# Keys in one tile, score products of up to 512 columns and another order of the head pairs in a streaming-encoder step

## The chip, the cores and the metric

The kernel runs on one core of one Trainium2 chip. The metric is device time in microseconds (us) of one execution; each kernel is run several times and the median is compared.

## What is computed

One layer of a streaming encoder, for a prompt of 1024 frames and a sample group of 64 frames, with 1024 model dimensions. The parts that the change touches are the two attentions behind the first projection:

```python
h = rms_norm(xp, g_norm1[l])
qa, ka, va, qb, kb, vb, logf = in_proj(h, w_in[l], b_f[l], g_qa[l], g_ka[l], g_qb[l], g_kb[l])
oa = chunk_band_attn_prompt(qa, ka, va, rel_bias[l])   # 8 heads: own 64-frame chunk + 8 before it, relative bias
ob = forget_attn_prompt(qb, kb, vb, logf)              # 8 heads: causal, bias = cum[t] - cum[s], cum = cumsum(logf)
xp = xp + jnp.concatenate([oa, ob], axis=-1) @ w_o[l]
```

Both are softmax(q k / 8 + bias) v with heads of 64 dimensions. After them come a cross attention into 256 memory tokens, whose keys and values are projected in this kernel, and a feed-forward block with a short convolution. The sample group goes through the same layer with cached keys and values. The normalised keys, the values, the gates' logarithms and the memory's keys and values are outputs too.

## The kernel before, in words

**Precision.** TensorE works on a rounded 32-bit type (F32R). To keep precision, each operand is split into a high part (rounded) and a low part (the rest). A projection is three products: high x high, low x high, high x low (`SPLIT`, or `TERMS` at the start). In the attention, head dimension 64 leaves half of the 128 rows of the array free. So a query tile holds the high part of the query in one half of the partitions and its low part in the other. The key tile has two planes (`z` or `m` = 0 and 1, high and low), each with the same keys in both halves. The second half is filled by a DMA from the first (line 485, `k<-k`). A score is then two products, one per plane. For the values, high and low stand side by side as 128 weight columns (`v[:, j, h]` is 2 x 64), and the result has 128 rows, whose two halves are added at the end (lines 743 and 744).

**Stages.** The 16 heads go in 8 pairs, in the order `PAIRS` (line 24): pairs 0 to 3 are band attention ("local"), 4 to 7 forgetting attention. For each pair, the projection runs over eight blocks of 128 frames (line 407, 24 products of 384 columns each), then once over the sample group (line 529). Between these products the attention of earlier blocks is woven in, up to one pair late: `substeps` hands out the scores of one unit, the values of the unit before and the turning of new queries and keys. A unit (`Attn`) is one head and 256 queries (two blocks `j`) of one group of keys `g`. When the last pair's projection has ended, its last units run beside the projection of the memory (line 802); then follow the samples' attention (class `Sample`, in the order `SAMPLES`, line 25), the output projection and the rest of the layer (lines 1156, 1445, 1481, 1703, 2027).

**Keys and values.** Two blocks make a `Group` (lines 330 to 334), whose key tile has 256 columns per plane and head. The pool holds five such tiles. `group_turn` (line 473) transposes queries and keys and writes the key planes (ScalarE line 482, VectorE line 484, DMA line 485).

**Scores** (`score`, line 659). For query block t the window of key blocks is the five newest for a local pair and all t + 1 for a forgetting pair, that is up to 640 or 1024 columns of the PSUM tile `S` of two banks. The products (line 682) go group by group with 256 columns, or 128 where the window begins or ends in the middle of a group. Then come: add the bias and find the row's extreme (VectorE line 685), the exponential with its sum (ScalarE line 687), division by the sum (GpSimd line 689). In forgetting pairs GpSimd prepares the bias first (lines 667, 668).

**Values** (`turn`, `sum`, lines 705 and 723). The probabilities are transposed (line 719) and split (lines 720, 721). A block in the window of both query blocks is multiplied with 256 columns, a block in only one of the windows with 128; `self.full` lists the former. Line 734 does high and low probabilities with all 128 value columns.

**Gates' sum** (`forget`, line 558). The running sum of the logarithms of the gates is a scan over the frames, with eight heads on eight partitions (line 602), for the prompt and for the sample with its cache. Its pieces are handed out from block 1 of pair 1 on (line 867). Pairs 4 to 7 need its result as bias (line 639) and per query (line 612).

**The order of instructions.** Everything up to the first product of the feed-forward part (`arranged`, line 1591) is put in order by a planner, `arrange` (line 2050). It goes through the instructions as the program lists them, gives each a price (`cost`, line 2077) and plans every engine and SyncE's queue of DMAs. An instruction can be planned when what it needs is done; of those that are ready, the one earliest in the program goes first. `before` holds what has to be done, `starts` what has to have begun. The result is only an order on each engine. What an instruction waits for on the chip is set by the data alone. All DMAs are issued by SyncE.

Of the kernel before, what the change touches and what calls it, by code (L numbers as in the profile page):

```python
# [15 lines left out]
P = 128  # L16
# [6 lines left out]
NF = 22  # L23
PAIRS = (0, 1, 2, 3, 4, 5, 6, 7)
SAMPLES = (4, 7, 5, 6, 0, 1, 3, 2)
# [16 lines left out]
def hybrid_step(ctx: ExitStack, tc: tile.TileContext, i: dict, o: dict):  # L42
# [285 lines left out]


    class Group:  # L330
        def __init__(self):
            self.k = wa.tile([P, 2, 2, 256], F32R, name="k", bufs=5)
            self.v = wa.tile([P, 2, 2, 2, 64], F32R, name="v", bufs=5)
            self.q = self.qk = None
# [223 lines left out]
    def forget():  # L558
# [36 lines left out]
        def scan(n):  # L595
            nonlocal lt, cs
            cs = wk.tile([P, N], F32, name="s", bufs=4)
            if n == N:
                lt = wk.tile([P, N], F32, name="s", bufs=4)
                nc.sync.dma_start(lt[:8, 0:T], i["clogf"])  # L600
                dve.tensor_copy(lt[:8, T:N], ls)
            dve.tensor_tensor_scan(cs[:8, :n], lt[:8, :n], lt[:8, :n], 0.0, op0=ALU.add, op1=ALU.bypass)
            dve.tensor_scalar(lt[:8, :n], cs[:8, :n], -1.0, None, op0=ALU.mult)
            nc.sync.dma_start(negc if n == T else negs, lt[:8, :n])
# [37 lines left out]
    mixes = {}  # L642

    class Attn:

# [13 lines left out]
        def score(self, j, sp=None):  # L659
# [11 lines left out]
            else:  # L671
                b = bias[p, h][:, 640 - n:640]
            if sp is None:
                sp = ps.tile([P, 2, 512], F32, name="S", bufs=1).rearrange("p a b -> p (a b)")
            off = (w0 % 2) * P
            q = groups[p, g].q[:, h, j * P:(j + 1) * P]
            for kg in range(w0 // 2, t // 2 + 1):
                k0, k1 = max(w0, 2 * kg), min(t, 2 * kg + 1) + 1
                a = off + (k0 - w0) * P
                src = slice((k0 - 2 * kg) * P, (k1 - 2 * kg) * P)  # L680
                for m in range(2):
                    pe.matmul(sp[:, a:a + (k1 - k0) * P], q, groups[p, kg].k[:, h, m, src], start=m == 0, stop=m == 1)  # L682
            mx = wk.tile([P, 1], F32, name="mx", bufs=4)
# [39 lines left out]
        def sum(self, ch):  # L723
# [5 lines left out]
            op = self.op  # L729
            for b in sorted(ch, key=lambda b: (b != self.full[0], b)):  # L730
                cols = slice(0 if b <= a1 else 1, 2 if b >= b0 else 1)
                hi, lo, x = self.pts[b]
                for m, pt in enumerate((hi, lo)):
                    pe.matmul(op[:, cols], groups[p, b // 2].v[:, b % 2, h].rearrange("p a d -> p (a d)"),  # L734
                              pt[:, x, cols], start=b == self.full[0] and m == 0, stop=b == self.last and m == 1)
            if ch[-1] != self.last:
# [107 lines left out]
    for p, np_ in zip(PAIRS, PAIRS[1:] + (None,)):  # L844
# [5 lines left out]
        for t in range(NT):  # L850
# [13 lines left out]
            if t == 0:  # L864
                subs = extra[:1] + subs[:2] + extra[1:] + subs[2:]
                extra = []
            elif forgetting:
                subs += forgetting.pop(0)
# [1177 lines left out]

ENGINES = ("PE", "DVE", "Activation", "Pool", "SP")


def arrange(tc, end):  # L2050
# [6 lines left out]
    setter = select = None  # L2057
    held, slots = [], {}

# [17 lines left out]
    def cost(ins, engine, kind, cols, rows, psum):  # L2077

        op = str(getattr(ins, "op", ""))
        if engine == "PE":  # L2080
            if getattr(ins, "is_transpose", False):
                return 0.109, 0.35, False
            if ins.ins[0].bass_ap.dtype == F32:
                o = max(0.214, cols * 0.00178)
            else:
                o = max(0.087, 0.003 + cols * 0.000456)
            return o, o + 0.16, False
# [19 lines left out]
    for ins in traced[:end]:  # L2107
# [57 lines left out]
        if engine == "Pool":  # L2165
# [6 lines left out]
            elif kind == "InstTensorScalarAffineSelect":  # L2172
                select = n
        before.discard(n)
        nodes.append((ins, engine, before, starts, *cost(ins, engine, kind, cols, rows, psum)))
        held.append((olds, mine))

# [164 lines left out]
```

## Time and profile before

| | |
|---|---|
| median of the runs | 1707.46 us (3 runs, 1704.11 to 1709.73) |
| the profiled execution | 1703.21 us |
| its span, first to last instruction | 1701.4 us |
| mean clock granted to TensorE | 0.998 of full |

PE is TensorE, PEld its weight loads, DVE VectorE, ACT ScalarE, POOL GpSimd, SP SyncE; SPq and the like are an engine's sequencer, which waits or issues DMAs. L407 is line 407. A group of instructions is written as line, engine, operation, output<-inputs by the program's names, shape and count; for a product, 128*128 is the weights' rows and columns and 128x384 the moving operand. Behind the bar stand the busy time in us, the mean duration of one in ns, and the engine's idle time just before them with what ended it. Products overlap, so their durations say less than the distance between their starts. The chain of work that ended last follows the run back from its end, at each step to what released it; its pieces are given as start, length and what it is.

### The profile page before, as it was taken

To read this page: it belongs to the slowest core of one execution; us is meant where nothing else is said; L and a number is where in the kernel's file an instruction comes from. 1 tells how busy PE (TensorE), PEld (TensorE's weight loads), DVE (VectorE), ACT (ScalarE), POOL (GpSimd) and SP (SyncE) were. 2 spreads that over 40 slices of the span, in tenths; PEclk is the share of its full clock that TensorE was granted. 3 is DMA by queue.
4 is the path that set the end of the run, shared out by engine and by line. 5 is a ranking of instruction groups with operands and counts; after the bars stand their busy time and mean duration, and the time that the engine had idled before them with its cause. 6 is when DMAs were issued, how large, how long until landed. Compare 5 with 4: busy or idle time off the path is not lost.

```text
span 1701.4 us, 33544 instructions
## 1 busy us (share of the span) xinstructions
PE 1676.9 (99%) x12264; PEld 1636.4 (96%) x12264; DVE 1158.1 (68%) x2552; ACT 906.8 (53%) x1995; POOL 583.3 (34%) x846
## 2 busy tenths in 40 slices
PE   8999999999999999999999999999999999999999
PEld 8899999999998889999999999999999999999998
DVE  7877766767777645334444697777777777659986
ACT  8757766767777565335555554333333333434442
POOL 1746647888877104434445211000000000000000
PEclk9999999999999999999999999999999999999999
DMA  8322223223146955411114642222222222983332
GB/s 258 101 57 81 75 81 103 76 77 99 48 147 189 267 186 185 139 57 51 55 58 141 211 134 83 80 78 79 77 77 77 77 79 82 306 305 122 104 108 88
DMA packets 138422, 199.84 MB, mean 117 GB/s; under 512 B 22200, under 2 KB 77624, under 8 KB 138256
## 3 DMA queue, kind: packets, MB, share of 16 engines
q1 hardware_dynamic: 138256, 197.70, 37.8%
q8 instruction: 96, 1.57, 0.4%
q14 instruction: 70, 0.57, 0.1%
HBM read 148.01 MB, written 43.34 MB: 112 GB/s over the span
## 4 chain that ended last, share of the span: by engine, by line
PE 83%; DVE 6%; ACT 5%; DMA 2%; issue 2%; POOL 1%; SPq 0%; DVEq 0%; ACTq 0%; POOLq 0%
PE W L1703 26%; PE pj L1156 14%; PE W L2027 11%; PE pj L407 11%; PE S L682 4%; PE O L734 3%; PE PT L719 3%; PE pj L802 2%; PE W L1156 2%; PE pj L529 1%; PE S L1445 1%; PE tq L1481 1%; PE O L1481 1%; PE O L1056 1%; ACT q L487 1%
## 5 line engine op out<-in xcount | busy, mean ns | idle before, releaser
L407 PE MATMUL pj<-whi,xhi 128*128 128x384 f32 (+1 forms) x480 | 175.4, 365 | 0.0
L407 PE MATMUL pj<-wlo,xhi 128*128 128x384 f32 (+1 forms) x480 | 164.7, 343 | 0.0
L407 PE MATMUL pj<-whi,xlo 128*128 128x384 f32 (+1 forms) x480 | 164.1, 342 | 0.0
L1703 PE MATMUL W<-h,hi 128*128 128x272 f32 x704 | 134.3, 288 | 1.4 <-ACT qlo L1839 1.4
L1809 POOL COPY s<-gp 128x2 f32<-128x2 f32 x22 | 15.8, 719 | 336.1 <-DVE gp L1808 336.1
L2027 PE MATMUL W<-f,hi 128*128 128x272 f32 x672 | 127.2, 287 | 0.1
L721 DVE TENSOR_TENSOR ptl<-PT,pth 128x512 fp32r<-128x512 f32 (+2 forms) x192 | 98.5, 521 | 37.1 <-ACT pth L720 34.4
L720 ACT CAST pth<-PT 128x512 fp32r<-128x512 f32 (+2 forms) x192 | 85.2, 450 | 57.9 <-PE PT L719 55.8
L689 POOL TENSOR_SCALAR s<-s,ssum 128x640 f32<-128x640 f32 (+7 forms) x128 | 92.0, 720 | 69.5 <-DVE ssum L688 59.2
L687 ACT ACTIVATE s<-s,mx 128x640 f32<-128x640 f32 (+7 forms) x128 | 94.4, 737 | 37.6 <-DVE mx L685 36.9
L1703 PEld LDWEIGHTS W<-h,hi 128*128 128x128 f32 x704 | 110.4, 188 | 1.7 <-ACT qlo L1839 1.6
L2027 PEld LDWEIGHTS W<-f,hi 128*128 128x128 f32 x672 | 105.3, 188 | 0.3 <-DVE f L1774 0.3
L1703 PE MATMUL W<-h,lo 128*128 128x272 f32 x352 | 101.4, 288 | 0.0
L682 PE MATMUL S<-k,q 128*128 128x256 f32 (+1 forms) x608 | 94.3, 283 | 6.9 <-DVE mx L685 4.5
L682 PEld LDWEIGHTS S<-k,q 128*128 128x128 f32 x608 | 83.9, 190 | 17.2 <-DVE mx L685 5.6
L2027 PE MATMUL W<-f,lo 128*128 128x272 f32 x336 | 96.7, 288 | 0.0
L1566 ACT CAST hi<-raw 128x512 fp32r<-128x512 f32 x68 | 42.3, 621 | 98.8 <-PE W L1703 59.2
L719 PE MATMUL PT<-ident,s 128*128 128x128 f32 x528 | 89.8, 275 | 3.2 <-DVE ptl L721 1.5
L407 PEld LDWEIGHTS pj<-whi,xhi 128*128 128x128 f32 x480 | 90.9, 189 | 1.2
L407 PEld LDWEIGHTS pj<-wlo,xhi 128*128 128x128 f32 x480 | 91.2, 190 | 0.1
L407 PEld LDWEIGHTS pj<-whi,xlo 128*128 128x128 f32 x480 | 90.4, 188 | 0.0
L1156 PE MATMUL pj<-a,hi 128*128 128x384 f32 (+1 forms) x352 | 87.3, 332 | 1.0 <-DVE a L1209 0.9
(608 smaller groups left out, 5716.1 us busy)
## 6 DMA issues: line engine op xcount, KB each, us to landing
raw<-in_w_down_dram SPq DMA_DIRECT2D x45, 256.0 KB, 2.8
wraw<-in_w_dram SPq DMA_DIRECT2D x56, 192.0 KB, 2.7
raw<-in_w_up_dram SPq DMA_DIRECT2D x41, 256.0 KB, 2.7
h<-ad SPq DMA_DIRECT2D x32, 272.0 KB, 5.2
mwraw<-in_w_mkv_dram SPq DMA_DIRECT2D x16, 512.0 KB, 5.0
raw<-in_w_mo_dram SPq DMA_DIRECT2D x32, 256.0 KB, 3.3
kvraw<-in_w_down_dram SPq DMA_DIRECT2D x32, 256.0 KB, 2.7
k<-k SPq DMA_DIRECT2D x60, 128.0 KB, 2.3
```

What stands on the lines that cost most here:

```text
L407: pe.matmul(pj[:, :nw], x_part(a, k, t * P, P), wt[k][b][:, :nw], start=n == 0, stop=n == 3 * KT - 1)
L682: pe.matmul(sp[:, a:a + (k1 - k0) * P], q, groups[p, kg].k[:, h, m, src], start=m == 0, stop=m == 1)
L687: act.activation(s[:, :n], s[:, :n], ACT.Exp, bias=mx, scale=-1.0, accum_out=sm)
L689: pool.tensor_scalar(s[:, :n], s[:, :n], sm, 1.0, op0=ALU.mult, op1=ALU.mult)
L719: pe.transpose(pt[:, b - ch[0]], self.s[j][:, (b - w0) * P:(b - w0 + 1) * P], ident)
L720: act.copy(hi[:, f:f + n, j], pt[:, f:f + n])
L721: dve.tensor_tensor(lo[:, f:f + n, j], pt[:, f:f + n], f32(hi[:, f:f + n, j]), op=ALU.subtract)
L734: pe.matmul(op[:, cols], groups[p, b // 2].v[:, b % 2, h].rearrange("p a d -> p (a d)"), pt[:, x, cols], start=b == self.full[0] and m == ...
L1156: pe.matmul(out()[:, :cn], w[a][:, k % 4], x[b][k][:, c0:c0 + cn], start=k == 0 and (a, b) == SPLIT[0], stop=k == KT - 1 and (a, b) == SPL ...
L1566: act.copy(hi, t)
L1703: pe.matmul(w[:, z, :Q], a(p, j), rights[j][b][:, z * Q:z * Q + Q], start=fresh and begin and j == 0 and x == 0, stop=final and end and j ...
L2027: pe.matmul(ws[m][:, z, :Q], la[p][:, m * P:(m + 1) * P], ra[b][:, z * Q:z * Q + Q], start=first and y == 0 and what in opening, stop=fina ...
```

## The change

- `PAIRS`: pair 3 (local) goes last, behind the forgetting pairs 4 to 7. Two places that count along `PAIRS` move with it: the memory's statistics, in block 4 of the fourth pair, now fall into pair 4; what is put beside the last pair's blocks (memory loads and splits) now falls into pair 3. The pieces of the gates' sum are handed out from pair 2 on (`p > 1`).
- All keys lie in one tile `ring` of five slots of 256 columns, which the groups take in turn.
- `key_parts` cuts the window of a query block into runs of blocks that lie side by side in the ring and stay within one PSUM bank, up to 512 columns; it tries each place in `S` and takes the cheapest, where a part counts as many blocks as it has, at least two. For the units that share one `S` tile at the start it keeps to the bank.
- In `sum`, a block that is not in `full` multiplies the low part of the probabilities with the high half of the values alone (64 weight columns instead of 128); the product of low and low is left out there. Such blocks go first, behind the one that opens the accumulation.
- The scan of the gates' sum is cut into four pieces of a quarter each, each starting from the end of the one before.
- In the planner, a product costs at least 0.87 ns for each weight column (before: 87 ns whatever the weights), and a DMA is not planned before the product that stands ten back in the program has begun.

```diff
-PAIRS = (0, 1, 2, 3, 4, 5, 6, 7)
+PAIRS = (0, 1, 2, 4, 5, 6, 7, 3)
...
+    RING = 5
+    ring = wa.tile([P, 2, 2, RING * 256], F32R, name="k")
+    turns_of = []
...
-            self.k = wa.tile([P, 2, 2, 256], F32R, name="k", bufs=5)
+            self.at = len(turns_of) % RING
+            turns_of.append(self)
+            self.k = ring[:, :, :, self.at * 256:self.at * 256 + 256]
...
-            dve.tensor_tensor_scan(cs[:8, :n], lt[:8, :n], lt[:8, :n], 0.0, op0=ALU.add, op1=ALU.bypass)
+            for a in range(0, n, n // 4):
+                c = slice(a, a + n // 4)
+                dve.tensor_tensor_scan(cs[:8, c], lt[:8, c], lt[:8, c], cs[:8, a - 1:a] if a else 0.0, op0=ALU.add, op1=ALU.bypass)
...
+    def key_parts(p, w0, t, bank_only):
+
+        where = [groups[p, b // 2].at * 256 + b % 2 * P for b in range(w0, t + 1)]
+        n = len(where)
+        best = None
+        for first in range(1 if bank_only else 9 - n):
+            cost, parts, x = 0, [], 0
+            while x < n:
+                m = 1
+                while x + m < n and where[x + m] == where[x] + m * P and (first + x + m) % 4:
+                    m += 1
+                parts.append(((first + x) * P, where[x], m * P))
+                cost += max(2, m)
+                x += m
+            if best is None or cost < best[0]:
+                best = cost, first * P, parts
+        return best[1:]
...
-            off = (w0 % 2) * P
             q = groups[p, g].q[:, h, j * P:(j + 1) * P]
-            for kg in range(w0 // 2, t // 2 + 1):
-                k0, k1 = max(w0, 2 * kg), min(t, 2 * kg + 1) + 1
-                a = off + (k0 - w0) * P
-                src = slice((k0 - 2 * kg) * P, (k1 - 2 * kg) * P)
-                for m in range(2):
-                    pe.matmul(sp[:, a:a + (k1 - k0) * P], q, groups[p, kg].k[:, h, m, src], start=m == 0, stop=m == 1)
+            off, parts = key_parts(p, w0, t, bank_only)
+            for a, k0, m in parts:
+                for z in range(2):
+                    pe.matmul(sp[:, a:a + m], q, ring[:, h, z, k0:k0 + m], start=z == 0, stop=z == 1)
...
-            for b in sorted(ch, key=lambda b: (b != self.full[0], b)):
+            steps = [(b, m) for b in sorted(ch, key=lambda b: (b in self.full, b)) for m in range(2)]
+            if first:
+                steps.sort(key=lambda x: x != (self.full[0], 0))
+            for b, m in steps:
                 cols = slice(0 if b <= a1 else 1, 2 if b >= b0 else 1)
-                hi, lo, x = self.pts[b]
-                for m, pt in enumerate((hi, lo)):
-                    pe.matmul(op[:, cols], groups[p, b // 2].v[:, b % 2, h].rearrange("p a d -> p (a d)"),
-                              pt[:, x, cols], start=b == self.full[0] and m == 0, stop=b == self.last and m == 1)
+                v = groups[p, b // 2].v[:, b % 2, h].rearrange("p a d -> p (a d)")
+                x = self.pts[b][2]
+                r = 64 if m and b not in self.full else P
+                pe.matmul(op[:r, cols], v[:, :r], self.pts[b][m][:, x, cols], start=first and (b, m) == steps[0], stop=ch[-1] == self.last and (b, m) == steps[-1])
...
-            elif forgetting:
+            elif forgetting and p > 1:
                 subs += forgetting.pop(0)
...
+AHEAD = 10
...
-                o = max(0.087, 0.003 + cols * 0.000456)
+                o = max(0.00087 * ins.ins[1].bass_ap.ap[1][1], 0.003 + cols * 0.000456)
...
+        if engine == "PE":
+            products.append(n)
+        if engine == "SP" and len(products) > AHEAD:
+            starts.add(products[-1 - AHEAD])
```

More of the change, by code (lines that the diff above doesn't have):

```diff
@@ L672, in score @@
                 b = bias[p, h][:, 640 - n:640]
+            bank_only = sp is not None
             if sp is None:
                 sp = ps.tile([P, 2, 512], F32, name="S", bufs=1).rearrange("p a b -> p (a b)")
-            off = (w0 % 2) * P
             q = groups[p, g].q[:, h, j * P:(j + 1) * P]
-            for kg in range(w0 // 2, t // 2 + 1):
-                k0, k1 = max(w0, 2 * kg), min(t, 2 * kg + 1) + 1
-                a = off + (k0 - w0) * P
-                src = slice((k0 - 2 * kg) * P, (k1 - 2 * kg) * P)
-                for m in range(2):
-                    pe.matmul(sp[:, a:a + (k1 - k0) * P], q, groups[p, kg].k[:, h, m, src], start=m == 0, stop=m == 1)
+            off, parts = key_parts(p, w0, t, bank_only)
+            for a, k0, m in parts:
+                for z in range(2):
+                    pe.matmul(sp[:, a:a + m], q, ring[:, h, z, k0:k0 + m], start=z == 0, stop=z == 1)
             mx = wk.tile([P, 1], F32, name="mx", bufs=4)
@@ L2057, in arrange @@
     setter = select = None
-    held, slots = [], {}
+    held, slots, products = [], {}, []
     def cells(t, offset, dims, dram):
```

## The prediction

> **What bounds the kernel now.** I read the page first, for the engines' shares and the chain that ended last.
>
> ```profile
> span 1701.4 us, 33544 instructions
> ...
> PE 1676.9 (99%) x12264; PEld 1636.4 (96%) x12264; DVE 1158.1 (68%) x2552; ACT 906.8 (53%) x1995; POOL 583.3 (34%) x846
> ...
> PE 83%; DVE 6%; ACT 5%; DMA 2%; issue 2%; POOL 1%; SPq 0%; DVEq 0%; ACTq 0%; POOLq 0%
> ```
>
> TensorE is busy all through and most of the chain is its own work. The change lies in the attention, so the next view was the table by stretches: the gates' sums (100 to 140 us), one pair of band attention (164 to 227), one forgetting pair (336 to 402) and the end of the last pair (520 to 560).
>
> ```profile
> core 0: us, PE busy (x) PEld busy (x) DVE busy (x) ACT busy (x) POOL busy (x), PEclk, DMA share, GB/s
> 100.00:120.00 20.00, 18.97 (x123) 17.27 (x122) 14.51 (x45) 11.15 (x35) 10.83 (x16) 1.00 0.12 31
> 120.00:140.00 20.00, 19.71 (x139) 18.30 (x137) 17.27 (x44) 15.61 (x39) 12.05 (x19) 1.00 0.21 52
> 164.00:227.00 63.00, 62.87 (x432) 60.74 (x432) 43.91 (x128) 44.00 (x116) 38.26 (x57) 1.00 0.26 72
> 336.00:402.00 66.00, 65.84 (x457) 63.41 (x455) 46.69 (x123) 45.82 (x115) 57.09 (x93) 1.00 0.31 83
> 520.00:540.00 20.00, 18.81 (x147) 17.81 (x147) 15.52 (x39) 14.12 (x38) 17.11 (x26) 1.00 0.67 184
> 540.00:560.00 20.00, 17.98 (x144) 16.73 (x144) 17.52 (x45) 13.79 (x33) 7.97 (x10) 1.00 1.02 289
> ```
>
> The second column is the stretch's length, then busy time of TensorE, its weight loads, VectorE, ScalarE and GpSimd. Inside a pair TensorE idles 0.13 us of 63 and 0.16 of 66: there a nanosecond off TensorE is a nanosecond off the kernel, as long as no other engine fills up. The fullest other one is GpSimd in a forgetting pair, 57.09 of 66, with 8.9 us free. At the two ends TensorE does wait: 1.03 + 0.29 us between 100 and 140, 1.19 + 2.02 us between 520 and 560. So the change can pay in two ways, by less TensorE work and by fewer waits at these places.
>
> **What a product costs.** The durations of single products overlap, so I take spacings, from runs of equal products in the chain (start, length, count) and in the timeline. The groups by shape give the counts (behind the x) and mean durations.
>
> ```profile
> 152.62 1.05 PE pj L407 x6
> ```
>
> ```profile
> 1018.39 447.65 PE W L1703 x3570
> ```
>
> ```profile
> 127.82 0.49 PE L719 MATMUL PT<-ident,s 128*128 128x128 f32 x3
> ```
>
> ```profile
> L682 PE MATMUL S<-k,q 128*128 128x256 f32 x448 | 76.4, 293 | 4.8 <-DVE mx L685 3.6 <-DVE q L489 0.2
> ...
> L682 PE MATMUL S<-k,q 128*128 128x128 f32 x160 | 28.2, 258 | 2.1 <-DVE mx L685 0.9 <-DMA k<-k 0.9 <-DVE q L374 0.3
> ...
> L734 PE MATMUL O<-ptl,v 128*128 128x128 f32 x80 | 22.1, 276 | 0.0
> ```
>
> L407's products have 384 moving columns and take 1.05 / 6 = 175 ns; L1703's have 272 and take 447.65 / 3570 = 125.4 ns. The slope is (175 - 125.4) / 112 = 0.443 ns a column, so 256 columns cost 118 ns, 512 cost 232 ns and 128 would stream in 62 ns. Three products of 128 columns last 0.49 us from the first's start to the last's end; one alone lasts 276 ns (last row): (0.49 - 0.276) / 2 = 107 ns each. A 128-column product therefore costs 107 and not 62, and since a product starts only when its weights are in, I take the next 128-column load to be what it waits for.
>
> **Wider score products.** Before, each query block goes over the keys group by group: 448 products of 256 columns and 160 of 128 (rows above). Working `key_parts` through with five slots and the new order of pairs (slots 0 1 2 3, then 4 0 1 2, 3 4 0 1, 2 3 4 0, 1 2 3 4, 0 1 2 3, 4 0 1 2, 3 4 0 1), splits remain where the slots wrap and at each 512 columns of PSUM. I count 192 of 256 columns, 96 of 384, 80 of 512 and 64 of 128; both counts cover 1056 blocks. Before: 448 x 0.118 + 160 x 0.107 = 70.0 us. After: 192 x 0.118 + 96 x 0.175 + 80 x 0.232 + 64 x 0.107 = 64.9 us. Gain **5.1 us**, nearly all from 128-column products that vanish into 384. No row shows 512 columns of this type. The nearest ones are these, and L407's.
>
> ```profile
> 583.10 1.88 PE L1018 MATMUL S<-kraw,sq 128*128 128x512 f32 x4
> ```
>
> They are plain 32-bit tiles, not the rounded type of the keys, at no more than 1.88 / 4 = 0.47 us. At that price 80 wide products cost 19.0 us more and the term turns to -13.9; at L407's 0.175 they cost 4.6 less and it is +9.7. I take 232, because L407 and L1703 are of the keys' type and L1018 is not.
>
> The Trainium skill ("TensorE: Matmul & The Clock Gate", section "Back-to-back issue gap") gives a sustained 81 ns at 128 columns and 131 ns at 512. By a line between these the term would be 11.3 us, an estimate from that page; but by that line 272 columns would take 100 ns, where 3570 products here take 125.4 each, so it is not used.
>
> A merged product needs all its keys at once, so the newest group's arrival now holds back up to three older blocks too, and behind it everything queued on TensorE. Keys arrive by the copy of line 485.
>
> ```profile
> PE S L682 <- DMA k<-k: 0.9, 1, 0.9
> ```
>
> TensorE waited for such a copy once in the whole run, 0.9 us, at the end of the last pair. Cost taken: 0; if that cover went, each late product would lose at most the older blocks' 0.35 us.
>
> **Narrow value weights.** For the 80 single-block products with the low half of the weights (row above), 64 instead of 128 columns of values are loaded. What a half load is worth shows where this kernel already has one of the same type:
>
> ```profile
> L1445 PEld LDWEIGHTS S<-kPh,qhi x48: 187/188/193, 744.6 to 898.3; 128*128 128x128 f32 x48
> ...
> L1445 PEld LDWEIGHTS O<-kSh,qhi x8: 133/134/135, 775.6 to 900.1; 128*64 128x64 f32 x8
> ```
>
> 188 - 134 = 54 ns less, so the load drops from 107 to about 53 and streaming, 62 ns, becomes the limit: 80 x (0.107 - 0.062) = **3.6 us**. Bounds: 0 if the loads are hidden anyway, 80 x 0.054 = 4.3. Below zero is excluded, since nothing is added.
>
> The Trainium skill ("TensorE: Matmul & The Clock Gate", section "Weight-path perf modes") speaks against this edit: a fast weight load is on only with 128 weights and a type other than FP32, so 64 columns would leave it. The rows disagree: here the 128-column load is the longer one by 54 ns.
>
> **The gates' sum in four pieces, and one pair later.**
>
> ```profile
> L602 DVE TENSOR_TENSOR_SCAN s<-s x2: 2268/2336/2403, 115.2 to 126.7; 8x1024 f32<-8x1024 f32 x1, 8x1088 f32<-8x1088 f32 x1
> ```
>
> ```profile
> 115.42 2.17 POOL m L351
> ...
> 126.75 2.32 DVE s L602
> ```
>
> The scans hold VectorE 2.3 us each and, the first one, a tiny GpSimd operation of four columns 2.17 us; both lie on the chain just ahead of TensorE's idle 1.32 us. Pieces of some 0.6 us let the urgent work between. Six more instructions cost VectorE perhaps 1.2 us, hidden in the 2.7 us it idles in the fuller of these stretches. They now run in pair 2, and pair 4 first reads their result a block of products (24 x 0.175 = 4.2 us) or more later. Gain **1.0 us** (bounds -1.3, if the waits only double in the new place, to 1.3).
>
> **Local pair last, and loads held back.**
>
> ```profile
> 528.20 3.14 DMA sv<-vf
> ...
> 531.87 0.60 SPq L974
> ...
> 532.56 3.52 DMA k<-k
> ```
>
> The last pair's drain has little projection work to hide under. Today it is a forgetting pair: GpSimd is at 17.11 of 20 us, a sample's cache load (L974) is issued on SyncE's queue just ahead of the key copy, which then takes 3.52 us, and sample 7, second in line, reads back what this pair has just stored (sv). With pair 3 there, GpSimd has a third less to do (38.26 against 57.09 above), the windows are at most 640 columns, and sample 3 comes seventh. The held-back rule adds no wait on the chip: it only changes the written order of SyncE's queue, so that key copies and stores pass loads that are not yet needed. Of the 3.2 us idle between 520 and 560 I take three quarters: **2.4 us** (0 to 3.2). The moved memory statistics (two squares and their loads) come into pair 4 and lie beside TensorE work; ScalarE idles 20 us there.
>
> **Sum.** 5.1 + 3.6 + 1.0 + 2.4 = 12.1 us. The profiled execution took 1703.2 us, 1.8 more than its span, and would come to 1691.1. The runs' median, 1707.5, is 4.3 above it; I subtract from that: **1695.4 us**.
>
> **Rivals.**
> 1. *Waits take the stall terms' place.* The order of the first 950 us is planned afresh, so waits can appear anywhere. The two TensorE terms, 8.7, stay; the stall terms give nothing and 3 us of new waits arise, about as much as the drain has today: 1701.8. For it: GpSimd's 87% in forgetting pairs. Against: the 0.16 us idle there.
> 2. *TensorE's gain is eaten.* Waits worth 8 us, GpSimd's 2 in each of the four forgetting pairs, with no stall term: 1706.8. Against: it has 8.9 us free in each, and a pair loses only (5.1 + 3.6) / 8 = 1.1 us of cover.
> 3. *Slower: the key tile binds.* If one tile's writes and reads waited for each other as a whole, every turn of a group would stop scores from the first key write to the landing of the copy.
>
> ```profile
> k<-k SPq DMA_DIRECT2D x60, 128.0 KB, 2.3
> ```
>
> Two copies a turn make 30 turns; 2.3 us each (the median from issue to landing), half covered by projections, is 34.5 us: 1729.9. It decides from 12.1 / 30 = 0.40 us uncovered a turn. Against it:
>
> ```profile
> 31.32 0.50 ACT L373 ACTIVATE k<-O,gd 128x256 fp32r<-128x256 f32 x1
> ...
> 32.88 0.41 PE L682 MATMUL S<-k,q 128*128 128x128 f32 x2 [0.31 <-DVE q L374]
> ...
> 34.59 0.48 DVE L374 SCALAR_TENSOR_TENSOR k<-O,gd,k 128x256 fp32r<-128x256 f32 x1
> ```
>
> The score of block 0 ran between the two writes of block 1's keys, which stand ahead of it in the program and go to the same group's tile. Parts are told apart.
> 4. *Wide products at another price*: at 0.175 us, 1690.8; at 0.47, 1714.4.
> 5. *Narrow loads bring nothing*: 1699.0.
>
> **How the numbers follow.** Forecast 0.65; rival 1 0.15; rival 2 0.09; rival 3 0.05; rival 4 0.02 for cheap and 0.01 for dear; rival 5 0.03. About 0.3%, 5.1 us, is what a measurement of this kernel can tell: faster is below 1702.3, slower above 1712.6. Faster: 0.65 + 0.02 + 0.03 and half of rival 1, 0.78. Same: the rest of rival 1 and rival 2, 0.16. Slower: rival 3 and the dear products, 0.06. All upper bounds at once (9.7 + 4.3 + 1.3 + 3.2 = 18.5) give 1689.0; with the runs' spread of about 2 the low end is 1687. The high end is rival 1 with that spread, 1704; what lies outside is rivals 2 and 3 and the dear products.
>
> **What would show it.** Right: 432 score products in four widths, 512 columns spaced by some 232 ns; 80 weight loads of 64 columns near 134 ns; TensorE's idle time inside pairs unchanged, and under 1 us in the 40 us before the last pair's end; scans of some 0.6 us. Wrong: 512-column products beyond 0.3 us, score products waiting for key writes, or GpSimd as releaser in the forgetting pairs.

## The result, and the profile after

The changed kernel takes 1696.62 us (median of 6 runs, 1692.34 to 1698.63); the kernel before took 1705.78 us beside it (6 runs, 1702.28 to 1710.38). The ratio is 0.9943, with a 95% interval of 0.9928 to 0.9959: 0.57%, or 9.7 us of 1705.78 (7.0 to 12.3 by the interval). Forecast were 12.1 us less, and 1695.4 us. The profiled execution took 1696.54 us (before: 1703.21). Three executions in all, the longest of 9205 us, took far longer than the others of their kernel and are left out of every median here.

The page of the changed kernel, engines' shares and chain:

```profile
span 1694.7 us, 33145 instructions
...
PE 1668.7 (98%) x12088; PEld 1622.9 (96%) x12088; DVE 1155.8 (68%) x2558; ACT 906.8 (54%) x1995; POOL 582.9 (34%) x846
...
PE 63%; DVE 1%; DMA 1%; ACT 1%; issue 1%; DVEq 0%; ACTq 0%
```

There are 176 products fewer, and TensorE is busy for 1676.9 - 1668.7 = 8.2 us less, while the span is 6.7 us shorter. So TensorE idles slightly longer than before, 26.0 against 24.5 us. That already says where the forecast went wrong: the work disappeared, the waits did not. (The chain's shares are not to be compared with those of before: they add up to 67%, since this chain is followed back only to about 557 us.)

The groups by shape of the changed kernel (score products, and the value products with narrow weights):

```profile
L706 PE MATMUL S<-k,q 128*128 128x256 f32 x192 | 36.4, 288 | 0.6 <-DVE mx L709 0.2
L706 PE MATMUL S<-k,q 128*128 128x384 f32 x96 | 26.3, 355 | 3.8 <-DMA k<-k 2.0 <-DVE mx L709 1.4 <-DVE q L495 0.4
L706 PE MATMUL S<-k,q 128*128 128x512 f32 x80 | 25.5, 408 | 1.9 <-DVE mx L709 1.1 <-DVE q L495 0.7
L706 PE MATMUL S<-k,q 128*128 128x128 f32 x64 | 12.1, 271 | 0.7 <-DMA k<-k 0.2 <-DVE q L495 0.2
...
L762 PEld LDWEIGHTS O<-ptl,v 128*64 128x64 f32 x80 | 10.9, 136 | 0.2
L762 PE MATMUL O<-ptl,v 128*64 128x128 f32 x80 | 18.4, 230 | 0.0
```

The counts are the 192, 96, 80 and 64 of the prediction, and the 80 narrow loads last 136 ns. None of these groups waits for a write of keys; the only waits for keys are those for the copy, 2.2 us in all. What one costs is read from the distance between starts, in the timeline of TensorE:

```profile
259.92 0.22 PE L762 MATMUL O<-ptl,v 128*64 128x128 f32 x1
259.98 0.33 PE L762 MATMUL O<-pth,v 128*128 128x256 f32 x1
...
498.84 0.63 PE L706 MATMUL S<-k,q 128*128 128x512 f32 x2
499.31 0.34 PE L413 MATMUL pj<-whi,xlo 128*128 128x384 f32 x1
```

Two products of 512 columns take 0.47 us up to the next start, 235 ns each (forecast 232). A narrow product takes 0.06 us (forecast 62 ns). Over all 80 of each the median distance to the next start is 233 and 59 ns; for the same low product with 128 weight columns, in the kernel before, it was 111. The Trainium skill ("TensorE: Matmul & The Clock Gate", section "Back-to-back issue gap") gives a sustained 131 ns at 512 columns; for this type the measurement decides, and it is 235.

Next, four stretches of the changed kernel that answer to those of the prediction: the 40 us from the start of pair 1's projection, pair 2 with the gates' sums, a forgetting pair, and the 40 us up to the last pair's end (columns as in the prediction):

```profile
95.38:135.38 40.00, 39.85 (x268) 37.82 (x268) 27.93 (x83) 29.64 (x79) 25.82 (x40) 1.00 0.30 79
155.40:218.40 63.00, 60.98 (x402) 55.99 (x402) 49.04 (x134) 41.20 (x109) 43.04 (x65) 1.00 0.33 88
322.12:387.64 65.52, 65.12 (x426) 61.52 (x426) 45.80 (x123) 46.16 (x116) 57.05 (x93) 1.00 0.31 84
507.28:547.28 40.00, 37.58 (x285) 35.49 (x284) 33.05 (x90) 29.46 (x80) 15.54 (x25) 1.00 0.59 165
```

And the 40 us up to the last pair's end in the kernel before:

```profile
519.08:559.08 40.00, 36.78 (x289) 34.53 (x288) 32.90 (x82) 27.94 (x70) 25.93 (x38) 1.00 0.83 232
```

The place from which the gates' sums were taken idles 0.15 us (before: 1.32 between 100 and 140), but pair 2, to which they went, now idles 2.02 us where a local pair idled 0.13. The forgetting pair idles 0.40 us (before 0.16). At the last pair's end 2.42 us are idle instead of 3.22; under 1 was expected.

Whole stages next: up to the last of the sample's products of the second pair, to the last of those of the eighth, and to the first product of the output projection. The stages do not hold the same work in two kernels (the first has 800 products before and 754 after), since each kernel is planned anew. Kernel before:

```profile
0.00:136.42 136.42, 126.05 (x800) 117.80 (x801) 105.21 (x306) 101.55 (x269) 65.29 (x98) 0.99 0.45 133
136.42:524.37 387.95, 386.51 (x2652) 371.66 (x2651) 272.36 (x757) 274.81 (x704) 295.04 (x467) 1.00 0.32 89
524.37:631.65 107.28, 101.66 (x756) 91.32 (x755) 64.30 (x176) 63.84 (x170) 25.20 (x43) 0.98 0.79 229
```

Changed kernel:

```profile
0.00:127.53 127.53, 120.85 (x754) 114.47 (x755) 98.73 (x299) 101.23 (x268) 63.76 (x97) 0.99 0.46 136
127.53:519.57 392.04, 387.63 (x2557) 365.89 (x2557) 281.35 (x772) 276.00 (x703) 305.33 (x480) 1.00 0.32 87
519.57:622.20 102.63, 95.57 (x720) 85.65 (x719) 59.71 (x173) 62.80 (x173) 15.67 (x31) 1.00 0.84 248
```

The second and the third row are to be read together, because the exchange of pairs moves forgetting work from the last stage into the middle one. The first stage gains 8.9 us, the two others together 495.23 - 494.67 = 0.56 us, and the rest of the kernel, whose code is the same, takes 2.7 us more (1701.4 - 631.65 = 1069.8, and 1694.7 - 622.20 = 1072.5). Of the 2.7, 1.7 are a stretch of half clock at 626 us (last section); the kernel before has such a stretch too, but in its last stage, at 568 us. In the last stage TensorE is idle 7.06 us instead of 5.62, although the stage is shorter.

What takes the place of the old waits there is shown by the chain of the changed kernel, cut to the memory stage (start, length, what):

```profile
576.30 6.03 DMA mwraw<-in_w_mkv_dram
...
586.84 4.79 DMA mwraw<-in_w_mkv_dram
...
592.90 0.48 PE O L1083 x2
```

In this stretch the chain runs along loads of the memory's weights. The waits of ScalarE between 510 and 640 us name them too (us in total, times, longest):

```profile
ACT mwhi L821 <- DMA mwraw<-in_w_mkv_dram: 6.0, 3, 4.0
```

The kernel before has no such wait. The last pair's last product starts 11.8 us earlier than before (547.28 us against 559.08), and the last of the 16 loads is issued at the same time (588.28 us, before 588.71).

The opening, finally. SyncE's queue in the kernel before:

```profile
23.68 2.00 SPq L128 DMA_DIRECT2D wraw<-in_w_dram  x4
...
30.75 0.44 SPq L635 DMA_DIRECT2D bias<-rows  x1
```

and in the changed kernel:

```profile
26.01 0.44 SPq L643 DMA_DIRECT2D bias<-rows  x1
...
27.77 2.15 SPq L128 DMA_DIRECT2D wraw<-in_w_dram  x4
```

The order is turned round: the biases that the first scores need now go out ahead of the next weights, 4.7 us earlier. VectorE waited 2.5 us for them before and does not wait for them now. No step of the prediction had this. That it is the held-back rule's doing, the runs with and without it show below.

### The profile page after: what moved, and what is told of

Same layout as the page of the kernel before. It is cut to its first block, busy times and chain, and to the rows that moved or that the text cites. A ratio compares the mean times of both kernels' runs of the same rounds, so it can differ in the third digit from the quotient of the medians.

```text
span 1694.7 us, 33145 instructions
## 1 busy us (share of the span) xinstructions
PE 1668.7 (98%) x12088; PEld 1622.9 (96%) x12088; DVE 1155.8 (68%) x2558; ACT 906.8 (54%) x1995; POOL 582.9 (34%) x846
## 4 chain that ended last, share of the span: by engine, by line
PE 63%; DVE 1%; DMA 1%; ACT 1%; issue 1%; DVEq 0%; ACTq 0%
PE W L1730 26%; PE pj L1183 14%; PE W L2054 14%; PE W L1183 2%; PE pj L829 1%; PE S L1472 1%; PE tq L1508 1%; PE O L1508 1%; DMA mwraw<-in_w_mkv_dram 1%; PE PT L1495 1%; PE O L1083 1%; PE O L1472 1%; PE PT L1183 0%; PE PT L1453 0%; PE S L1045 0%
## 5 line engine op out<-in xcount | busy, mean ns | idle before, releaser
L706 PE MATMUL S<-k,q 128*128 128x256 f32 (+3 forms) x432 | 90.4, 323 | 7.0 <-DVE mx L709 2.8
L706 PEld LDWEIGHTS S<-k,q 128*128 128x128 f32 x432 | 67.2, 188 | 21.5 <-DVE q L495 8.4
```

What stands on the lines that cost most here:

```text
L706: pe.matmul(sp[:, a:a + m], q, ring[:, h, z, k0:k0 + m], start=z == 0, stop=z == 1)
```

## The experiments

All were timed beside the kernel before. Ratios are to that kernel, with their 95% intervals. As in the change itself, the narrow weights leave out the product of low probabilities and low values; nothing else is left out anywhere.

### The two edits on TensorE alone

The kernel before with the key tile, the wide score products and the narrow weights; order of pairs, gates, scans and planner as before.

```diff
-PAIRS = (0, 1, 2, 4, 5, 6, 7, 3)
+PAIRS = (0, 1, 2, 3, 4, 5, 6, 7)
...
-            elif forgetting and p > 1:
+            elif forgetting:
...
-        if engine == "SP" and len(products) > AHEAD:
-            starts.add(products[-1 - AHEAD])
```

> The kernel before with the two edits of TensorE's work alone: keys in one tile with score products of up to 512 columns, and 64 weight columns for the low part of single blocks (the product of low and low is left out there, as in the change). Order of pairs, place and form of the gates' sum and the planner are those of before. The forecast's theory: the two terms, 5.1 + 3.6 = 8.7 us, are paid in full, so about 8.7 us under the kernel before. Rival (waits eat TensorE's gain): the fresh plan puts new waits between the products, and less than 5 us are left.

Measured: 1695.09 us, ratio 0.9940 (0.9928 to 0.9953), 10.2 us less (8.0 to 12.3). The two edits alone give as much as the whole change, as far as the intervals tell. Its stages:

```profile
0.00:135.04 135.04, 125.13 (x769) 116.82 (x770) 105.45 (x307) 101.58 (x268) 63.66 (x97) 0.97 0.47 135
135.04:520.02 384.98, 382.31 (x2510) 360.51 (x2509) 271.61 (x755) 274.18 (x703) 295.21 (x467) 1.00 0.32 89
520.02:624.88 104.86, 100.20 (x741) 89.08 (x740) 64.81 (x178) 65.02 (x171) 28.05 (x44) 1.00 0.83 234
```

Against this kernel the whole change is 7.5 us ahead after the first stage, loses 494.67 - 489.84 = 4.8 us in the two next ones and about 3 us behind them. Of the 7.5, 3.2 are idle time of TensorE (9.91 against 6.68 us) and 1.7 clock: here the granted clock is 0.50 from 35.4 to 42.2 us, in the changed kernel only from 59.8 to 63.2.

### Scores by group, and wide value weights

The changed kernel with one of the two edits undone each: first the products group by group over the same key tile, second `r = P`.

```diff
-            off, parts = key_parts(p, w0, t, bank_only)
-            for a, k0, m in parts:
+            off = (w0 % 2) * P
+            for kg in range(w0 // 2, t // 2 + 1):
+                k0, k1 = max(w0, 2 * kg), min(t, 2 * kg + 1) + 1
```

```diff
-                r = 64 if m and b not in self.full else P
+                r = P
```

> The changed kernel with the score products cut group by group again (448 of 256 columns, 160 of 128), the keys still in the one tile. The forecast's theory: 5.1 us over the changed kernel. Rival (other work covers it): under 2 us, since the planner fills TensorE otherwise and the waits shrink as the products grow.

> The changed kernel with all 128 weight columns in every value product again, in the new order of blocks. The forecast's theory: 80 products at 107 instead of 62 ns, 3.6 us over the changed kernel. Rival (the loads are mostly hidden): the high product before each takes part of the load, so that 2 us or less remain.

Measured: by group 1704.28 us, 0.9995 (0.9981 to 1.0008); wide values 1704.79 us, 0.9993 (0.9982 to 1.0003). Each gives back nearly the whole gain, 8 to 9 us against the changed kernel. The middle stage, by group and with wide values:

```profile
128.26:527.28 399.02, 393.18 (x2700) 373.31 (x2699) 280.88 (x771) 276.76 (x701) 303.94 (x479) 1.00 0.31 86
```

```profile
126.51:522.54 396.03, 391.44 (x2556) 367.80 (x2556) 281.51 (x773) 275.72 (x702) 304.83 (x479) 1.00 0.31 86
```

TensorE's busy time there rises by 5.6 and by 3.8 us over the changed kernel's 387.63, which is the size forecast for each term (5.1 and 3.6, for the whole kernel). The remaining 3 us of the one and 4 of the other are only in part accounted for. By group, TensorE idles 28.3 us in the whole trace against 26.0, and 3.4 us more of the trace run at half clock, worth 1.7 us. The trace of the wide values, from an execution of 1701.31 us, has as much half clock, but less idle time (24.2 us) than the changed kernel's. The two losses add up to 16 us, more than the two edits gain together, so single prices found in this way can't be added.

### Local pair not last

```diff
-PAIRS = (0, 1, 2, 4, 5, 6, 7, 3)
+PAIRS = (0, 1, 2, 3, 4, 5, 6, 7)
```

> The changed kernel with the pairs in the old order, 0 to 7, and nothing else undone. The forecast's theory: the drain of a forgetting pair comes back, about 2.4 us over the changed kernel, with GpSimd and the key copy as releasers between 510 and 560 us. Rival (the drain's wait only moved): no difference beyond 1 us, since what the last pair's end saves is given back in the memory stage behind it.

Measured: 1702.25 us, 0.9975 (0.9962 to 0.9988), 5.6 us more than the changed kernel. The exchange does matter in the changed kernel. The waits of the kernel without it from 510 us on are, above all, ScalarE's for memory weights, 8.3 us, and TensorE's behind them:

```profile
563.11 1.14 ACT L821 CAST mwhi<-mwraw 128x512 fp32r<-128x512 f32 x2 [3.51 <-DMA mwraw<-in_w_mkv_dram]
566.90 0.62 ACT L821 CAST mwhi<-mwraw 128x512 fp32r<-128x512 f32 x1 [2.65 <-DMA mwraw<-in_w_mkv_dram]
```

```profile
564.55 0.33 PE L1022 MATMUL tq<-ident,sqd 64*128 64x64 f32 x2 [1.65 <-DVE smx L1050]
...
570.35 2.08 PE L1045 MATMUL S<-kraw,sq 128*128 128x512 f32 x2 [4.04 <-ACT sq L1027]
```

The number in square brackets is the idle time just before the instruction. The sample's `sq` (569.99 us), for which TensorE waits 4.04 us, comes on ScalarE behind the split of a memory weight that had not landed. The windows show the clock beside these waits:

```profile
560.00:566.11 6.11, 4.46 (x32) 3.70 (x30) 3.93 (x11) 1.14 (x2) 2.43 (x7) 1.00 0.97 295
566.11:576.35 10.24, 6.20 (x18) 3.83 (x17) 5.25 (x19) 4.37 (x14) 1.73 (x3) 0.50 0.96 264
```

The granted clock is 0.50 for 10.24 us. It falls behind the first of the two waits, of 1.65 us, and the second lies inside the stretch; TensorE is busy there for 6.20 us at half clock.

### Without the held-back rule, and with the rule alone

The first is the changed kernel without the rule, the second the two edits on TensorE with the rule added.

```diff
-        if engine == "SP" and len(products) > AHEAD:
-            starts.add(products[-1 - AHEAD])
```

```diff
+        if engine == "SP" and len(products) > AHEAD:
+            starts.add(products[-1 - AHEAD])
```

> The changed kernel without the planner's rule that holds DMAs back until the product ten back has begun. The forecast's theory: the rule is part of the 2.4 us gained at the end of the last pair, so without it the kernel is up to 1 us slower, with longer key copies there. Rival (the rule makes loads late): in the trace of the changed kernel ScalarE waits 4.03 us for a load of memory weights at 591.7 us, and TensorE 2.27 us behind it; without the rule this wait goes, and the kernel is 2 to 3 us faster than the changed one.

> The kernel with TensorE's two edits alone, and the held-back loads. What the runs so far say: the rule's gain lies in the opening (start to the first sample product 65.1 us without it against 62.3 in the changed kernel), so 2.5 to 3 us less there; but with a forgetting pair last it makes the loads for the samples late (116.8 us from the eighth sample product to the output projection in the kernel with the old order, against 102.6), so 5 us or more are lost there and the kernel is 2 to 7 us slower than with the two edits alone. Rival (the rule only helps): 2.5 us faster than with the two edits alone, the late stage unchanged.

Measured: without the rule 1698.84 us, 0.9959 (0.9946 to 0.9972), 2.2 us above the changed kernel, with intervals that overlap. Its first stage takes 131.59 us instead of 127.53. VectorE waits 3.3 us for the opening's biases. In the four traces without the rule in the opening it waits 1.8 to 4.0 us for them, and in the ten with it not at all. That the rule makes the memory's loads late falls as a cause for the changed kernel: without it ScalarE still waits 3.7 us for them (6.0 with it), and TensorE's wait behind ScalarE, 2.27 us at 592.9 us in the changed kernel, is 2.36 at 596.0. With the rule alone 1699.06 us, 0.9958 (0.9947 to 0.9970), 3 to 4 us more than without it (by the ratios or by the medians). Its first and last stage show both sides:

```profile
0.00:128.43 128.43, 120.83 (x759) 112.22 (x760) 103.35 (x303) 99.17 (x265) 64.00 (x94) 1.00 0.47 135
...
512.62:627.11 114.49, 104.81 (x743) 91.79 (x743) 66.05 (x179) 67.36 (x176) 27.76 (x47) 0.96 0.79 222
```

The first stage is 135.04 - 128.43 = 6.6 us shorter than without the rule, the last one 114.49 - 104.86 = 9.6 us longer. Part of both is clock (the column behind the five engines): 3.4 us of the 6.6, since this trace has no half clock in its opening, and 5.1 of the 9.6. TensorE's idle time alone is 2.3 us less and 5.0 us more. Here, behind a forgetting last pair, ScalarE waits 5.1 us for memory weights that no one waited for without the rule. The rule is good in one place and bad in another.

### The local pair last, alone

The two edits on TensorE with the new order of pairs.

```diff
-PAIRS = (0, 1, 2, 3, 4, 5, 6, 7)
+PAIRS = (0, 1, 2, 4, 5, 6, 7, 3)
```

> The kernel with TensorE's two edits alone, and the local pair last. The forecast's theory: most of the 2.4 us of the drain, so about 2 us under the kernel with the two edits alone; from the eighth sample product to the output projection (104.9 us there) at least 2 us less. Rival (the gain is bound to the held-back loads): no difference beyond 1 us.

Measured: 1700.99 us, 0.9970 (0.9959 to 0.9981): 5 to 6 us more than the two edits without it, where less was expected. So the exchange by itself does not pay; it pays beside the rule (5.6 us above). ScalarE waits for memory weights here as well, 2.6 us.

### The gates' sums back in pair 1, and scans in one piece

```diff
-            elif forgetting and p > 1:
+            elif forgetting:
```

```diff
-            for a in range(0, n, n // 4):
-                c = slice(a, a + n // 4)
-                dve.tensor_tensor_scan(cs[:8, c], lt[:8, c], lt[:8, c], cs[:8, a - 1:a] if a else 0.0, op0=ALU.add, op1=ALU.bypass)
+            dve.tensor_tensor_scan(cs[:8, :n], lt[:8, :n], lt[:8, :n], 0.0, op0=ALU.add, op1=ALU.bypass)
```

> The changed kernel with the gates' sum handed out from pair 1 on again, still in four pieces. The forecast's theory: the pieces, not the place, make the gain of 1.0 us, so no difference beyond 1 us. Rival (the place matters and was moved to a worse one): the waits of more than 0.13 us in pair 2 of the changed kernel add up to 3.8 us where they were 0.8 before; with the sum back in pair 1 they fall below 1.5 there, pair 1 gains less than 2, and the kernel is 1 to 2 us faster than the changed one.

> The changed kernel with each scan of the gates' sum in one piece again, still in pair 2. The forecast's theory: the four pieces are worth 1.0 us, so about 1 us slower, with the waits in pair 2 growing from 3.8 to 5 us. Rival: the pieces bring nothing in pair 2 (four of 0.74 us take VectorE longer than one of 2.3), no difference beyond the scatter, and pair 2's waits stay or fall.

Measured: in pair 1, 1696.34 us, 0.9945 (0.9933 to 0.9958), no difference to the changed kernel. From the sample of the first pair to that of the second it takes 2.7 us more, from there to the third pair's 2.4 us less. Single scans: 1698.64 us, 0.9960 (0.9946 to 0.9974), not told apart from the changed kernel. Pair 2, between the last sample products of the second and the third pair, in the kernel before, the changed kernel and the one with single scans:

```profile
136.42:199.37 62.95, 62.82 (x432) 60.44 (x431) 43.06 (x129) 43.64 (x116) 37.77 (x56) 1.00 0.27 72
```

```profile
127.53:193.43 65.90, 63.95 (x416) 58.42 (x416) 48.18 (x135) 42.10 (x113) 38.75 (x56) 1.00 0.30 75
```

```profile
128.65:192.80 64.15, 63.26 (x413) 58.21 (x412) 46.43 (x129) 42.49 (x113) 37.70 (x56) 1.00 0.29 77
```

TensorE idles 0.13, 1.95 and 0.89 us there, so the pieces gain nothing in pair 2. The other traces of this document, each with a plan of its own, agree on the place: pair 2 idles 1.3 to 3.2 us in the seven kernels that run the pieces in it, and 0.1 to 0.6 in the six that run the sums in pair 1. Pair 1 idles 1.2 to 2.2 us with the sums in it and 0.4 to 1.2 without. The cost was moved, not removed.

### Another plan with the same program

The planner's price of a semaphore signal is raised, which changes nothing but the planned order.

```diff
-    signal = 0.07
+    signal = 0.08
```

> The changed kernel with one number of the planner altered: the time that it assumes for a signal between engines, 0.08 instead of 0.07 us. No work is added or removed; only the order on the engines can change. If the differences of 3 to 6 us between the kernels so far beyond TensorE's own work are luck of the plan (a wait falling here or there, and with it a window of 3.4 us at half clock), this kernel moves by 2 us or more, up or down. If they come from the edits, it stays within 1 us of the changed kernel.

Measured: 1696.60 us, 0.9950 (0.9934 to 0.9966), in total the same. Inside, the first stage is 1.6 us shorter and the last 3.2 us longer than in the changed kernel, and ScalarE waits 14.1 us for memory weights instead of 6.0. Two stretches of half clock, worth 3.4 us together, lie in that last stage, and none lies in the changed kernel's. Differences of a stage of 3 us can therefore not be put down to an edit by itself, and with one altered plan that is a lower bound.

### The held-back rule in the opening only

The rule for the first 1000 products, once with the two edits on TensorE alone, once in the changed kernel.

```diff
+        if engine == "SP" and AHEAD < len(products) < 1000:
+            starts.add(products[-1 - AHEAD])
```

```diff
-        if engine == "SP" and len(products) > AHEAD:
+        if engine == "SP" and AHEAD < len(products) < 1000:
```

> The kernel with TensorE's two edits alone, and the held-back loads only for the first 1000 products (pairs 0 and 1 and half of pair 2). If the rule's gain lies in the opening and its cost behind the last pair: start to the second sample product 127 us instead of 133.7, late stage as with the two edits alone (104.9), about 5 us faster than these, 1690. If the late stage is planned anew by every edit: the opening's gain shows, but the sum is anywhere from 1690 to 1697.

> The changed kernel with the held-back loads only for the first 1000 products. If the rule is useless or harmful behind the opening: no slower than the changed kernel, up to 3 us faster. If it helps at the last pair's end as the forecast had it: 1 to 3 us slower, with the late stage (102.6 us in the changed kernel, 105.5 without the rule) back at 105.

Measured: 1692.53 us, 0.9926 (0.9912 to 0.9940), and 1697.85 us, 0.9953 (0.9940 to 0.9967). The first has the lowest median of all: by the ratios 2.4 us below the two edits alone and 2.9 below the changed kernel, with intervals that overlap; against the kernel before it is 12.6 us. Part of this may be clock: the mean clock of its runs is 0.9996, that of the two edits alone 0.9988. Its stages:

```profile
0.00:131.88 131.88, 123.54 (x760) 115.06 (x761) 102.28 (x303) 99.46 (x265) 64.15 (x94) 0.99 0.45 132
131.88:518.53 386.65, 383.34 (x2520) 361.65 (x2519) 272.12 (x760) 275.82 (x706) 297.99 (x469) 1.00 0.32 91
518.53:623.67 105.14, 100.36 (x741) 89.06 (x740) 64.00 (x178) 65.14 (x171) 26.62 (x44) 1.00 0.83 234
```

The first stage keeps 135.04 - 131.88 = 3.2 us of the gain (1.7 of them clock), the last is within 0.3 us of the kernel without the rule, and no one waits for memory weights. In the changed kernel the same limit brings ScalarE's wait down from 6.0 to 0.4 us, but not the time: that wait is not what its total hangs on.

TensorE's idle time, which leaves out that products run slower at half clock, sorts all fourteen traces by edit, whatever their plans. Up to the last sample product of the first pair it is 5.2 to 6.6 us in the ten kernels with the rule there and 7.2 to 8.2 in the four without. In the last stage it is 4.7 to 5.6 us in the three with a forgetting pair last and no rule there, 6.1 to 9.3 in the nine with the local pair last, with the rule or without, and 9.7 and 11.0 in the two with a forgetting pair last and the rule.

## Why the prediction came out as it did

**Wider score products, narrow value weights: right.** Counts and prices are as forecast (medians of 233 ns for 232 and 59 for 62), and the two alone took 10.2 us off (ratio 0.9940, 0.9928 to 0.9953), where 5.1 + 3.6 = 8.7 was forecast; the interval, 8.0 to 12.3 us, holds that. The picture behind the second price is not quite right. The prediction has a product wait for the next 128-column load, but the load behind the low product has 128 columns in both kernels, and the high product just before it took 59 ns before and takes 60 now. What held is the price of the two together: 59 + 111 = 170 ns before, 60 + 59 = 119 now. Which load holds up which product is not shown. Late keys, put at a cost of 0, did cost something: TensorE waits 2.2 us in all for the key copy, where it waited 0.9 before, nearly all of it at products of 384 columns. In the traces with wide products this wait is 0.5 to 2.9 us, by group 0.4, so how much of it the wider products cause is not shown. The rivals on wide products at another price and on narrow loads without effect fall with this. So does the one on the key tile: no score product waits for a key write. Rival 2 asked for 2 us of waits in each forgetting pair; the one shown has 0.40, and none of the four more than 0.5.

**The gates' sum in four pieces, and one pair later: wrong.** The step that failed is "Pieces of some 0.6 us let the urgent work between". The pieces are there, and GpSimd's small operation is no longer held up for 2 us, but TensorE waits in the new place as it did in the old, and the pieces take longer together. (Three kernels with single scans have none of 2 us either: no such operation falls beside a scan in the traces of the two edits alone, of the local pair last alone and of the single scans above.) The scans and GpSimd's operation in the changed kernel:

```profile
L610 DVE TENSOR_TENSOR_SCAN s<-s x8: 666/740/1010, 172.3 to 191.5; 8x256 f32<-8x256 f32 x4, 8x272 f32<-8x272 f32 x4
```

```profile
L357 POOL TENSOR_SCALAR m<-m,eps x68: 260/272/697, 42.1 to 523.9; 128x4 f32<-128x4 f32 x60, 64x4 f32<-64x4 f32 x8
```

The eight pieces keep VectorE busy for 6.1 us, the two single scans for 4.7; TensorE's idle 1.95 us in pair 2 lie in the pair where the pieces run. Pair 1 gained about what pair 2 lost (1.6 and 1.8 us of idle time); of 1.0 us nothing is left. That the pieces' longer total is what makes TensorE wait is likely, but not shown.

**Local pair last, and loads held back: wrong in how it works, nothing left of 2.4 us.** The step that failed is "Of the 3.2 us idle between 520 and 560 I take three quarters": 0.8 us of idle time went instead of 2.4, and the key copy did not get ahead as it was to. "Key copies and stores pass loads that are not yet needed" came true only in part. The copy does pass the loads of the samples' cache (without the rule they stand ahead of it, and TensorE waits 2.18 us), but not the memory's. SyncE's queue and TensorE in the changed kernel:

```profile
521.29 0.90 SPq L813 DMA_DIRECT2D mwraw<-in_w_mkv_dram  x2
523.50 1.78 SPq L491 DMA_DIRECT2D k<-k  x2
```

```profile
529.20 0.62 PE L706 MATMUL S<-k,q 128*128 128x384 f32 x2 [1.68 <-DMA k<-k]
```

Two loads of 512 KB go out right ahead of the key copy, and TensorE waits 1.68 us for it (before 0.86). What the last pair's end does gain, 0.8 us of idle time, is lost again in the last stage as a whole, where TensorE idles 7.06 us against 5.62: the memory's part begins earlier and then waits for its weights. Against the three traces with a forgetting pair last and no rule there (4.7 to 5.6 us) the exchange is no gain in any of the nine that have it (6.1 to 9.3 us); it is one only against the two that have the rule as well (9.7 and 11.0). The rule's true gain lies in the opening, which the prediction did not look at, and its harm behind a forgetting last pair.

**Where the gain went.** Term by term 8.7 + 1.0 + 2.4 was forecast. Measured are 10.2 for the first, and for the rest nothing that shows: the two edits alone stand at 0.9940, the whole change at 0.9943, and two such ratios leave some 3 us either way. So these runs alone would hardly rule out the 3.4 us of the stall terms; that they were not paid as forecast rests on the idle times above. Inside that nothing stand 7.5 us gained in the first stage, 1.7 of them clock, and about as much lost behind it. This is rival 1 as to the stall terms, which gave nothing. Its 3 us of new waits did not come in full: all of TensorE's idle time rose by 1.5 us, 24.5 to 26.0.

That 1696.62 us lies so near to the forecast of 1695.4 is in part luck. The gain was 2.4 us smaller than forecast, but the sum starts from 1707.46 us, the median of three runs, and the kernel before took 1705.78 in six, 1.7 less.

**The clock.** Part of the differences is the granted clock. The changed kernel's fastest run took 1692.34 us at a mean clock of 1.000, its longest 1698.63 at 0.997. Over the 51 runs of the kernel before, 0.001 of mean clock went with 1.1 us. If all of the time went with the clock, it would be 1.7. Mean clocks were 0.9982 for the changed kernel, 0.9966 with the local pair fourth, 0.9964 with wide values. By these two rates 1.8 to 2.7 us of the 5.6 between the first two are clock, and 2.0 to 3.1 of the 8.2 between the first and the last. That is an estimate from means: no run here set the clock by itself. The traces show the same in steps: apart from the very end of the span, the time at half clock is 6.8 us in the changed kernel (two stretches of 3.4), 10.2 with wide values (6.8 and 3.4) and 20.5 with the local pair fourth (3.4, 6.8 and 10.2).

**What stays open.** Which edit sets how long TensorE idles in the last stage is told by the three groups above, which do not overlap; which single wait makes up the difference is not. Nor is it settled why undoing one edit on TensorE costs 8 us where its price is 4 to 5: each run is also a new plan of the first 950 us, and has its own clock.

## What to carry to other kernels

Here work taken off an engine that is busy 98% of the time paid what was forecast, within the interval, and it could be priced beforehand from spacings in the trace. A change of order is worth what the whole kernel says, not what the place shows at which it was aimed: the waits here moved to the next load that was not early enough. A rule for a whole queue is best tried stage by stage; held back in the opening, the loads helped; held back throughout, behind a forgetting last pair, they cost more than they gave. And a difference of a few us between two traces is read with the clock beside it: idle time and clock first, then time.

## What was new of the hardware

The granted clock falls to half for a few us after TensorE has been short of work. The changed kernel has such a place at 626 us:

```profile
620.00:640.00 20.00, 18.90 (x100) 16.64 (x101) 16.30 (x44) 17.05 (x51) 5.66 (x4) 0.91 0.53 168
...
623.00:626.00 3.00, 2.05 (x9) 1.11 (x8) 3.00 (x7) 2.95 (x9) 2.02 (x2) 1.00 1.02 337
626.00:630.00 4.00, 4.00 (x18) 3.76 (x18) 2.80 (x7) 3.51 (x10) 1.28 (x1) 0.57 0.22 79
```

A mean of 0.91 over 20 us is 0.09 x 20 = 1.8 us lost, or 3.6 us at half clock. In the 3 us ahead of it TensorE was idle for 0.95 us only. In all fourteen traces the stretches at 0.50 in the span's first 1000 us last 3.4, 6.8 or 10.2 us, and in the 3.4 us ahead of each TensorE was idle for 0.95 to 2.6 us. The Trainium skill ("TensorE: Matmul & The Clock Gate", Part 1) gives about 3.4 us as the length of a window of the clock gate, with half rate behind an idle one; the trace agrees with the length, but less than a whole window of idle time was enough here. So a wait in a kernel that is bound by TensorE can cost its own length and some 1.7 us more: the 1.65 us wait above was followed by 10.24 us at half clock, with the 4.04 us wait among them and TensorE busy for 6.20.

A scan has a fixed part: 2268 ns for 1024 elements a row and 740 for 256 (a median that has pieces of 272 in it) make 1528 / 768 = 2.0 ns an element and some 230 ns at the start. And while a single scan ran in the kernel before, GpSimd's operation of four columns took 2165 ns, against a median of 272 (2167 and 2169 in two other traces with single scans, each time beside the scan); beside the pieces of the changed kernel its longest is 697 ns.
